# The low halves of one weight split of each gate and up pair, subtracted on GpSimd and not on VectorE

## The chip, the cores and the metric

The kernel runs on one core of one Trainium2 chip. The metric is device time in microseconds (us) of one execution; the time before is the median of three runs. Engine names are short: PE is TensorE (PEld its weight loads), DVE is VectorE, ACT is ScalarE, POOL is GpSimd, SP is SyncE, which issues most transfers.

## The reference

The network is a decoder trunk of two layers over 512 tokens of width 1024, in float32. Each layer has a mixer (a diagonal state space model, S5, beside chunked retention), a cross attention to a memory of 256 tokens, and a SwiGLU feed-forward part (FFN) of width 2816. The change concerns the last:

```python
D_MODEL, SEQ, DEPTH = 1024, 512, 2
D_FF = 2816

def rms_norm(x, g):
    y = x * lax.rsqrt(jnp.mean(x * x, axis=-1, keepdims=True) + EPS)
    return y * g

def swiglu(h, w_gate, w_up, w_down):
    return (jax.nn.silu(h @ w_gate) * (h @ w_up)) @ w_down

for l in range(DEPTH):
    ...                      # mixer, cross attention
    h = rms_norm(x, norm_ffn[l])
    x = x + swiglu(h, w_gate[l], w_up[l], w_down[l])
return rms_norm(x, norm_final)
```

## The kernel before

Activations lie transposed: 128 channels on the partitions, the 512 tokens along the free side. The matmuls run in a reduced form of float32 (fp32r), so every operand is split in two: a high part, which is the value copied to fp32r on ACT, and a low part, the value minus the high part, which DVE subtracts. A product takes three matmuls: high by high, high by low, low by high.

The FFN goes over its 2816 columns in four parts per layer (`FPARTS`: three of 6 blocks of 128 columns and one of 4). In a part the gate and up projections come first, then the down projection of the same columns. Gate and up use a Strassen-like scheme with seven products in place of eight: two neighbouring blocks of columns make a *pair* (one `gate` key and one `up` key for every two blocks, so 6 pairs in a part of 6 blocks, 4 in one of 4, 44 in the whole program). The sums of the weights that this scheme needs are formed on chip, in `prep_pair`, from two transfers `a` and `b` of 128 by 1024 each. Out of them come four *weight splits*, each a high and a low tile: `wa` (from `a`), `wb` (from `b`), `wc` (half as wide, from a sum) and `wd` (from another sum). For a pair DVE does four additions or subtractions of 128x512 on the raw tiles (shown as `raw<-raw` or `raw<-raw,raw`), three low parts of 128x1024 and one of 128x512 (`w<-raw,w`). ACT does the four high parts (`w<-raw`).

`pair_steps` then runs seven steps of 12 matmuls of 128x256, 84 for a pair (`ps<-u_nff,w`). Steps 0 and 1 read `wa`, 2 and 3 `wb`, 4 `wc`, 5 and 6 `wd`. `run_pairs` weaves the pairs into each other: the first three steps of the next pair stand between the last ones of this pair. After the steps, results are gathered from PSUM by ACT and DVE (`keep`: `u_gs<-ps,u_gs`, `u_us<-ps,u_us`), and the gating is done on DVE and ACT (`gated`, `merged`).

Buffers set what can run ahead: five tiles `raw` and eight tiles `w` of 128x1024. One pair takes all eight `w`, in a fixed turn, so a split of the next pair can be prepared only when PE has let go of the same split of this one.

The order of instructions on each engine isn't written by hand. The program records all operations, and a planner (`Program.schedule`) sorts them by due times, from a price for each operation (`price`: for a `tensor_tensor` on POOL 365 + 2.2 ns per element, on DVE 68 + 1.042 ns). Each engine then runs its list strictly in that order and waits on semaphores. Nothing in the prices ties one engine's duration to another's.

All instructions are issued at one helper (line 405 in the profile), so the rows tell operations apart by tile names. POOL has little to do: constants, S5 scalars at the start, S5 buffers and transfers in the mixers and in the FFN of the first layer, and four multiplications of the output (`u_fin`) at the end.

Of the kernel before, what the change touches and what calls it, by code (L numbers as in the profile page):

```python
# [10 lines left out]
F32 = mybir.dt.float32  # L11
# [406 lines left out]
def trunk(ctx, tc, io):  # L418
    nc = tc.nc
    mul, add, sub = ALU.mult, ALU.add, ALU.subtract  # L420
# [20 lines left out]
    V, S, G = Engine(prog, "DVE"), Engine(prog, "ACT"), Engine(prog, "POOL")  # L441
# [10 lines left out]
    def gen(s, dt=F32):  # L452
        return prog.buf("u", s, dt)
# [47 lines left out]
            finish()  # L501
        return ready.pop(i)

    def parts_of(x, s, n):
        hi, lo = prog.buf("w", s + "h"), prog.buf("w", s + "l")
        S.activation(out=hi[:, :n], in_=x, func=AF.Copy)
        V.tensor_tensor(out=lo[:, :n], in0=x, in1=hi.bitcast(F32)[:, :n], op=sub)
        return hi, lo

    def prep_pair(at):  # L510

        i = place[at]
        h = 512
        a, b = prog.buf("raw", "pa"), prog.buf("raw", "pb")
        Q.dma_start(out=a, in_=io["ws"][i, 0])
        Q.dma_start(out=b, in_=io["ws"][i, 1])
        V.tensor_tensor(out=b[:, :h], in0=b[:, :h], in1=b[:, h:], op=add)
        wa = parts_of(a, "wa", 2 * h)  # L520
        wb = parts_of(b, "wb", 2 * h)
        finish()
        V.tensor_tensor(out=b[:, :h], in0=b[:, :h], in1=a[:, :h], op=add)
        V.tensor_tensor(out=a[:, :h], in0=b[:, :h], in1=b[:, h:], op=sub)
        wc = parts_of(b[:, :h], "wc", h)

        def last():
            V.tensor_tensor(out=a[:, h:], in0=a[:, h:], in1=b[:, :h], op=add)
            ready[at] = (wa, wb, wc, parts_of(a, "wd", 2 * h))
        held.append(last)  # L530

    def finish():
        while held:
            held.pop()()
# [106 lines left out]
    for i in range(KT):  # L641
        Q.dma_start(out=xs[i], in_=io["xT"][:, i, :])
        raw, hi, lo = gen("w0")[:, :256], gen("w0h", F32R)[:, :256], gen("w0l", F32R)[:, :256]
# [1161 lines left out]
```

## Time and profile before

| quantity | before |
|---|---|
| median of 3 runs | 1473.82 us (1472.47 to 1475.63) |
| profiled execution, its own time | 1476.17 us |
| its span, first to last instruction | 1474.4 us |
| PE busy, of the span | 1453.7 us (99%) |
| DVE busy | 1192.1 us (81%) |
| ACT busy | 798.6 us (54%) |
| POOL busy | 97.9 us (7%) |
| TensorE clock granted, mean | 0.995 of full speed |

Busy shares are means over stages that differ. The table by windows cuts the span into stretches and gives the busy time and number of instructions of each engine in each; the table of groups gives the mean duration of one instruction of a kind. Consecutive instructions of DVE and of POOL overlap by some 0.05 to 0.1 us in the records, so what one instruction costs its engine is the distance from its start to the next start. Spans on POOL are called rough by the page, one more reason to go by the distances between starts. "ps" is a tile in PSUM, all other tiles lie in SBUF.

### The profile page before, as it was taken

The page shows a single profiled execution, that of the slowest core. Times are in us where ns is not written, and L with a number is a line of the kernel's source. Part 1 is how long each engine was busy: PE and PEld are TensorE (multiplying, and loading weights), DVE is VectorE, ACT ScalarE, POOL GpSimd, SP SyncE. Part 2 cuts the span into 40 slices and gives each one's busy share as a digit, 9 for nine tenths or more (in the row PEclk, how much of TensorE's full clock was granted, in tenths as well). Part 3 has the DMA queues.
Part 4 walks back from the last instruction along what each step waited for, and adds up shares of the span by engine and source line. Part 5 has one row for each costly group of instructions (what it writes and reads, how often), then busy time and mean ns, then how long its engine had stood idle before and what let it go on. Part 6 is the DMA issues. An engine that isn't in the chain of part 4 may idle for free.

```text
span 1474.4 us, 23052 instructions
## 1 busy us (share of the span) xinstructions
PE 1453.7 (99%) x8784; PEld 1279.2 (87%) x8784; DVE 1192.1 (81%) x2072; ACT 798.6 (54%) x1375; POOL 97.9 (7%) x201
## 2 busy tenths in 40 slices
PE   8999999999999999999999999999999999999997
PEld 6888788888898998998988888888889989999897
DVE  8799996576899797997963989756679969869596
ACT  5887665444665463564645436544455626436264
POOL 5721000000001001011000000000000000000001
PEclk8999999999999999999999999999999999999999
DMA  7534534221134334244345453332121322413321
GB/s 256 155 89 106 178 131 151 100 72 58 44 118 150 106 124 139 87 153 151 132 148 172 145 164 124 134 129 86 58 72 60 117 96 87 151 55 125 100 87 58
DMA packets 67023, 171.95 MB, mean 117 GB/s; under 512 B 11232, under 2 KB 22880, under 8 KB 66912
## 3 DMA queue, kind: packets, MB, share of 16 engines
q1 hardware_dynamic: 63808, 159.98, 32.4%
q0 software_dynamic: 3104, 10.49, 2.6%
q8 instruction: 69, 1.13, 0.3%
q14 instruction: 42, 0.34, 0.1%
HBM read 156.02 MB, written 13.63 MB: 115 GB/s over the span
## 4 chain that ended last, share of the span: by engine, by line
PE 82%; DVE 12%; ACT 3%; issue 1%; DMA 0%; SPq 0%; DVEq 0%; ACTq 0%
PE ps L405 82%; DVE w L405 3%; DVE u_gs L405 1%; DVE raw L405 1%; ACT w L405 1%; DVE u_us L405 1%; DVE s L405 1%; DVE u_gw L405 1%; DMA x<-in_xT_dram 0%; DVE u_mt L405 0%; ACT u_vc L405 0%; DVE u_rr L405 0%; ACT u_v L405 0%; SPq L405 0%; DVE u_ry L405 0%
## 5 line engine op out<-in xcount | busy, mean ns | idle before, releaser
L405 ACT ACTIVATE w<-raw 128x1024 fp32r<-128x1024 f32 (+1 forms) x348 | 347.8, 1003 | 414.9 <-PE ps L405 339.8
L405 PE MATMUL ps<-u_nff,w 128*128 128x256 f32 x3696 | 440.6, 280 | 0.7 <-DVE w L405 0.5
L405 PEld LDWEIGHTS ps<-u_nff,w 128*128 128x128 f32 x3696 | 436.9, 188 | 4.7 <-DVE w L405 1.9
L405 DVE TENSOR_TENSOR w<-raw,w 128x1024 fp32r<-128x1024 f32 (+1 forms) x336 | 383.7, 1148 | 55.7 <-ACT w L405 55.3
L405 PE MATMUL ps<-u_acth,w 128*128 128x512 f32 (+1 forms) x768 | 223.7, 375 | 0.0
L405 PEld LDWEIGHTS ps<-u_acth,w 128*128 128x128 f32 x768 | 139.9, 188 | 26.3
L405 PE MATMUL ps<-u_nmh,w 128*128 128x512 f32 x480 | 158.5, 402 | 0.0
L405 PE MATMUL ps<-u_actl,w 128*128 128x512 f32 (+1 forms) x384 | 143.0, 376 | 0.4 <-DVE u_actl L405 0.4
L405 DVE TENSOR_TENSOR x<-ps,x 128x512 f32<-128x512 f32 x88 | 60.5, 688 | 100.8 <-PE ps L405 100.5
L405 PEld LDWEIGHTS ps<-u_nmh,w 128*128 128x128 f32 x480 | 91.3, 191 | 18.7
L405 PE MATMUL ps<-u_nml,w 128*128 128x512 f32 x240 | 95.6, 398 | 0.0
L405 PEld LDWEIGHTS ps<-u_actl,w 128*128 128x128 f32 x384 | 72.2, 188 | 14.4 <-DVE u_actl L405 1.4
L405 PE MATMUL ps<-u_nch,w 128*128 128x512 f32 x256 | 81.7, 393 | 0.0
L405 PE MATMUL ps<-u_xoh,w 128*128 128x512 f32 x256 | 80.7, 392 | 0.0
L405 DVE TENSOR_TENSOR raw<-raw 128x512 f32<-128x512 f32 x88 | 60.4, 687 | 7.5 <-DMA raw<-in_ws_dram 7.0
L405 DVE TENSOR_TENSOR raw<-raw,raw 128x512 f32<-128x512 f32 x88 | 60.1, 683 | 0.4
L405 DVE TENSOR_TENSOR u_gs<-u_gs,u_nfry 128x512 f32<-128x512 f32 x88 | 59.0, 681 | 0.3
L405 PEld LDWEIGHTS ps<-u_nch,w 128*128 128x128 f32 x256 | 48.1, 188 | 10.4
L405 POOL TENSOR_TENSOR u_fin<-u_lp,u_lbc 128x512 f32<-128x512 f32 x4 | 5.4, 1392 | 775.3 <-ACT u_lbc L405 775.3
L405 PEld LDWEIGHTS ps<-u_xoh,w 128*128 128x128 f32 x256 | 48.0, 188 | 9.9
L405 PEld LDWEIGHTS ps<-u_nml,w 128*128 128x128 f32 x240 | 45.8, 191 | 9.4
L405 PE MATMUL ps<-u_xol,w 128*128 128x512 f32 x128 | 50.4, 393 | 0.0
(368 smaller groups left out, 2466.0 us busy)
## 6 DMA issues: line engine op xcount, KB each, us to landing
raw<-in_w_dram SPq DMA_DIRECT2D x166, 512.0 KB, 3.4
raw<-in_ws_dram SPq DMA_DIRECT2D x88, 512.0 KB, 3.5
u_s5x<-sp SPq DMA_DIRECT2D x28, 256.0 KB, 4.1
w<-in_w_dram POOLq DMA_DIRECT2D x6, 512.0 KB, 6.9
u_mr<-in_memT_dram SPq DMA_DIRECT2D x12, 256.0 KB, 4.7
x<-in_xT_dram SPq DMA_DIRECT2D x8, 256.0 KB, 4.7
tu<-u_u SPq DMA_DIRECT2D x8, 256.0 KB, 3.8
u_ub<-tu SPq DMA_DIRECT2D x32, 64.0 KB, 3.5
```

The source lines that it names most:

```text
L405: getattr(engines[o.eng], o.fn)(**k)
```

## The change

`parts_of` gets an optional engine for the subtraction that makes the low part, and `prep_pair` passes POOL for the first split of each pair, `wa`. The high parts stay on ACT, the other three low parts on DVE.

```diff
-    def parts_of(x, s, n):
+    def parts_of(x, s, n, eng=None):
         hi, lo = prog.buf("w", s + "h"), prog.buf("w", s + "l")
         S.activation(out=hi[:, :n], in_=x, func=AF.Copy)
-        V.tensor_tensor(out=lo[:, :n], in0=x, in1=hi.bitcast(F32)[:, :n], op=sub)
+        (eng or V).tensor_tensor(out=lo[:, :n], in0=x, in1=hi.bitcast(F32)[:, :n], op=sub)
         return hi, lo
...
-        wa = parts_of(a, "wa", 2 * h)
+        wa = parts_of(a, "wa", 2 * h, G)
         wb = parts_of(b, "wb", 2 * h)
```

Since the planner prices the two engines differently, the order on all engines shifts in the FFN. In the rows below a tile's name carries its buffer's number, as in `w_113` or `raw_105`. On DVE, in the third part of the second layer's FFN (some 1318 to 1327 us in the trace), the second pair to be prepared has `raw_105` as its `a` and `raw_106` as its `b`. Before:

```order
L405 TENSOR_TENSOR u_us<-ps_116,u_us 128x256 [waits PE_49,Activation_49]
L405 TENSOR_TENSOR u_gs<-u_gs,u_nfry 128x512 [waits Activation_49]
L405 TENSOR_TENSOR w_113<-raw_105,w_112 128x1024 [waits DMAHW4_49,Activation_49]
L405 TENSOR_TENSOR w_109<-raw_106,w_108 128x1024 [waits PE_49,Activation_49]
L405 TENSOR_TENSOR raw_107<-raw_107 128x512 [waits DMAHW7_49]
L405 TENSOR_TENSOR raw_106<-raw_106,raw_105 128x512 [waits DVE_49]
L405 SCALAR_TENSOR_TENSOR u_gs<-ps_122,u_gs 128x512
L405 TENSOR_TENSOR w_111<-raw_103,w_110 128x1024 [waits PE_49,Activation_49]
L405 TENSOR_TENSOR raw_105<-raw_106 128x512 [waits DVE_49]
L405 TENSOR_TENSOR w_115<-raw_106,w_114 128x512 [waits PE_49,Activation_49]
```

And with the change, DVE at the same place:

```order
L405 TENSOR_TENSOR u_us<-ps_121,u_us 128x256 [waits PE_49,Activation_49]
L405 TENSOR_TENSOR u_gs<-u_gs,u_nfry 128x512 [waits Activation_49]
L405 SCALAR_TENSOR_TENSOR u_gs<-ps_122,u_gs 128x512 [waits PE_49]
L405 TENSOR_TENSOR u_gs<-u_gs,u_nfry 128x512 [waits DVE_49]
L405 TENSOR_TENSOR w_109<-raw_106,w_108 128x1024 [waits Activation_49]
L405 TENSOR_TENSOR raw_107<-raw_107 128x512 [waits DMAHW7_49]
L405 TENSOR_TENSOR raw_106<-raw_106,raw_105 128x512 [waits DMAHW4_49,DVE_49]
L405 TENSOR_TENSOR u_gs<-u_gs,u_nfry 128x512 [waits Activation_49]
L405 TENSOR_TENSOR w_111<-raw_103,w_110 128x1024 [waits PE_49,Activation_49]
L405 TENSOR_TENSOR raw_105<-raw_106 128x512 [waits DVE_49,Pool_49]
L405 TENSOR_TENSOR w_115<-raw_106,w_114 128x512 [waits PE_49,Activation_49]
```

The low part `w_113<-raw_105,w_112` has left DVE, two gating operations on `u_gs` have moved up into its place, and the write into `raw_105`, which POOL now reads, waits for POOL as well.

On POOL, at the border between the FFN of the first layer (after its last S5 transfer) and that of the second, the difference reads as follows (+ is new; before, nothing stood there up to the `u_fin` of the end):

```order
 L405 DMA sp_207<-u_dt 128x512
+L405 TENSOR_TENSOR w_110<-raw_103,w_111 128x1024
+L405 TENSOR_TENSOR w_110<-raw_105,w_111 128x1024
+L405 TENSOR_TENSOR w_110<-raw_106,w_111 128x1024
+L405 TENSOR_TENSOR w_109<-raw_107,w_108 128x1024
+L405 TENSOR_TENSOR w_115<-raw_104,w_114 128x1024
```

Each is the low part of one pair's `wa`; there are 44 of them in all.

## Rows read from the trace of the kernel before

**Rows 1.** The page's first part: busy time by engine.
```profile
PE 1453.7 (99%) x8784; PEld 1279.2 (87%) x8784; DVE 1192.1 (81%) x2072; ACT 798.6 (54%) x1375; POOL 97.9 (7%) x201
```

**Rows 2.** Windows inside the eight gate and up stages: length, engines' busy us.
```profile
405.00:455.00 50.00, 49.79 (x416) 49.01 (x415) 49.20 (x74) 32.84 (x56) 1.68 (x4) 1.00 0.37 123
...
692.00:725.00 33.00, 33.00 (x285) 33.00 (x284) 30.95 (x44) 19.89 (x34) 0.00 (x0) 1.00 0.33 115
...
1223.00:1273.00 50.00, 50.00 (x423) 49.73 (x422) 48.20 (x71) 30.30 (x49) 0.00 (x0) 1.00 0.38 128
...
1410.00:1440.00 30.00, 30.00 (x256) 30.00 (x255) 28.87 (x41) 18.30 (x29) 0.00 (x0) 1.00 0.30 104
sum 368.00, PE 367.32 PEld 364.03 DVE 358.48 ACT 230.53 POOL 3.66; mean PE 45.91 PEld 45.50 DVE 44.81 ACT 28.82 POOL 0.46
```

**Rows 3.** Head of the chain of waits over 1307 to 1367 us.
```profile
by line: PE ps L405 40.3%; DVE w L405 22.8%; DVE raw L405 11.2%; issue 9.6%; DVE u_gs L405 7.8%; DVE u_us L405 6.5%; DVE u_actl L405 1.6%; ACT w L405 0.1%; DVEq L405 0.1%; ACTq L405 0.0%
```

**Rows 4.** DVE in order of time from 1324 us: start, duration.
```profile
1324.02 1.21 DVE L405 TENSOR_TENSOR w<-raw,w 128x1024 fp32r<-128x1024 f32 x1
1325.15 0.68 DVE L405 TENSOR_TENSOR raw<-raw 128x512 f32<-128x512 f32 x1
```

**Rows 5.** POOL's own two-input operations, in order of time: start, duration.
```profile
62.17 0.62 POOL L405 TENSOR_TENSOR u_s5bb<-u_s5b,fr 128x256 f32<-128x256 f32 x1
62.75 0.62 POOL L405 TENSOR_TENSOR u_s5bt<-u_s5b,fi 128x256 f32<-128x256 f32 x1
...
1456.91 1.30 POOL L405 TENSOR_TENSOR u_fin<-u_lp,u_lbc 128x512 f32<-128x512 f32 x1 [775.34 <-ACT u_lbc L405]
1458.16 1.30 POOL L405 TENSOR_TENSOR u_fin<-u_lp,u_lbc 128x512 f32<-128x512 f32 x1
1459.41 1.49 POOL L405 TENSOR_TENSOR u_fin<-u_lp,u_lbc 128x512 f32<-128x512 f32 x1
1460.87 1.48 POOL L405 TENSOR_TENSOR u_fin<-u_lp,u_lbc 128x512 f32<-128x512 f32 x1
```

**Rows 6.** DVE beside those four `u_fin`, in order of time.
```profile
1458.44 1.30 DVE L405 TENSOR_TENSOR u_la<-u_la,u_lq 128x256 f32<-128x256 f32 x1 [0.48 <-ACT u_lq L405]
1459.67 0.41 DVE L405 TENSOR_TENSOR u_ly<-ps,x 128x256 f32<-128x256 f32 x1
1460.56 0.63 DVE L405 TENSOR_TENSOR u_la<-u_la,u_lq 128x256 f32<-128x256 f32 x1 [0.48 <-ACT u_lq L405]
...
1463.50 0.42 DVE L405 TENSOR_TENSOR u_la<-u_la,u_lq 128x256 f32<-128x256 f32 x1 [0.55 <-ACT u_lq L405]
```

**Rows 7.** A POOL operation inside a gate and up stage, and DVE beside it.
```profile
413.73 0.61 POOL L405 TENSOR_TENSOR u_diag<-s5d,eye 32x256 f32<-32x256 f32 x1
413.84 1.06 DVE L405 TENSOR_TENSOR raw<-raw 128x512 f32<-128x512 f32 x1
```

**Rows 8.** POOL and DVE waiting for each other in the first mixer.
```profile
63.59 2.58 DVE L405 SCALAR_TENSOR_TENSOR s<-s,gam 128x4 f32<-128x4 f32 x1 [0.78 <-ACT u_v L405]
65.28 0.87 POOL L405 TENSOR_TENSOR u_s5bt<-u_s5b,fi 128x256 f32<-128x256 f32 x1
66.22 1.83 POOL L405 TENSOR_TENSOR u_s5bb<-u_s5bb,u_s5bt 128x256 f32<-128x256 f32 x1
66.25 1.21 DVE L405 TENSOR_TENSOR w<-raw,w 128x1024 fp32r<-128x1024 f32 x1
```

**Rows 9.** DVE's groups that read PSUM, 1223 to 1273 us: count, busy, mean ns.
```profile
L405 DVE TENSOR_TENSOR u_us<-ps,u_us 128x256 f32<-128x256 f32 x6 | 2.5, 417 | 0.4 <-PE ps L405 0.3
L405 DVE TENSOR_TENSOR u_gs<-ps,u_gs 128x256 f32<-128x256 f32 x5 | 2.1, 415 | 1.0 <-PE ps L405 1.0
L405 DVE SCALAR_TENSOR_TENSOR u_gs<-ps,u_gs 128x512 f32<-128x512 f32 x3 | 2.0, 680 | 0.0
L405 DVE SCALAR_TENSOR_TENSOR u_us<-ps,u_us 128x512 f32<-128x512 f32 x2 | 1.4, 679 | 0.0
```

**Rows 10.** The pairs' matmuls over the whole span.
```profile
L405 PE MATMUL ps<-u_nff,w 128*128 128x256 f32 x3696 | 440.6, 280 | 0.7 <-DVE w L405 0.5
```

## The prediction

> **What bounds the kernel now.** I read the page's busy times first. PE is busy for 99% of the span, DVE for 81% [rows 1]. Taken alone, this says that PE sets the time and DVE has a fifth to spare, so that relief for DVE is worth little and a burden on it costs little. But both are means over unlike stages, and the change works only in the gate and up stages of the FFN. So I laid a window inside each of the eight. Together the windows are 368.00 us long; in them DVE is busy for 358.48 us, 97%, and idle for 9.52 us, while POOL works for 3.66 us [rows 2]. ACT, with 230.53 us, is no bound. The reader is to see that the fifth of DVE's time that is free lies elsewhere, in the down projections and the attention.
>
> Then I asked which wait ends last there. In the third part of the second layer the chain runs 40.3% through PE, but 22.8% through DVE's low parts (`w`), 11.2% through its weight sums (`raw`), and 15.9% through gating (`u_gs`, `u_us`, `u_actl`) [rows 3]. DVE carries half of the path while PE is hardly idle: the two are level. One pair costs PE 84 matmuls, at the best pace of the windows (285 in 33.00 us, 0.1158 us each [rows 2]) 9.73 us, and DVE has about 9.5 us of work in the same time (48.20 us in a window of 423 matmuls, five pairs). What DVE gains or loses per pair therefore counts in very different ways. A gain meets PE at once: all 3696 matmuls of the pairs take 440.6 us [rows 10] and at the best pace would take 428.0, so no relief here is worth more than 12.6 us. A loss counts nearly in full.
>
> **What leaves DVE.** One low part of 128x1024 per pair, 44 in all. From its start to the next start is 1.13 us [rows 4], so DVE sheds 1.13 us per pair.
>
> **What POOL takes on.** The same subtraction, 44 times. Before, POOL has no operation of 128x1024. Uncontended it has two of 128x512 at 1.25 us from start to start and one of 128x256 at 0.58 us [rows 5]. Four times the small one is 2.32 us, twice the large one 2.50, and the line through both ends at 2.59. The third `u_fin`, which shared its time with DVE, took 1.46 from start to start, doubled 2.92: the upper end. I take 2.55, between the two readings that start at the nearest size. For POOL's own load this is nothing (2.55 in 9.73 us), and its queue is nearly empty there; in the first layer S5 buffers and transfers stand between the new operations, but they fall into the down stages.
>
> The Trainium skill has another price for this step. Its page "GPSIMD Engine Reference" (3.1, Elementwise) gives 4497 ns for an fp32 `tensor_tensor` of 2048 elements per partition; half of it, an estimate, is 2.25 us. By it the sum below would be 37 x (2.25 - 0.10 - 1.13) - 9.5 = 28 us; the trace's distances of 1.25 us for 512 elements speak for the dearer one.
>
> **What it does to DVE.** This decides. While POOL works through its four `u_fin`, DVE's `u_la`, which has two inputs in SBUF, takes 1.30 us in place of 0.42. It starts at 1458.44 and ends at 1459.74, 0.28 us after the second `u_fin` has ended at 1459.46. The next one takes 0.63 and again ends 0.29 us after a `u_fin` (1460.90). Between them `u_ly`, with one input in PSUM, takes its usual 0.41 in the midst of a `u_fin` [rows 5, 6]. It is no matter of that stage: at 413.84 us, inside a gate and up stage, a `raw<-raw` takes 1.06 us in place of 0.68 beside POOL's `u_diag` [rows 4, 7]. And it works both ways: POOL's `u_s5bb` of 128x256, started just before a low part on DVE, takes 1.83 us and ends 0.59 us after it [rows 8]. So a DVE operation with two SBUF inputs and a POOL operation that reads SBUF exclude each other, each for its whole length, and DVE, being in order, stands still behind its own head.
>
> The Trainium skill's page "SBUF — State Buffer" (Who interferes with whom) calls the port pair of the two an exclusive lock, held for the whole instruction, for exactly this combination. If the port were shared instead, each would slow in proportion, which is the first rival; the two `u_la` that end 0.28 us behind a `u_fin` fit the lock.
>
> In the gate and up stages nearly all of DVE's work is of the kind that is held: 16 of the 71 instructions of one window read PSUM, of 0.42 to 0.68 us [rows 2, 9]. When POOL gets its turn at the end of a DVE operation, the next one can run beside it with a chance of 16 in 71, for about 0.45 us, so 0.10 us per POOL operation is hidden. The rest of 2.55, 2.45 us, is lost to DVE. Per pair: 2.55 - 0.10 - 1.13 = 1.32 us more.
>
> **The sum.** The eight windows hold 3117 matmuls, 37 pairs. The other seven of the 44 are prepared in the stretch before a stage, where DVE has time. 37 x 1.32 = 48.8 us; the 9.5 us that DVE idles in the windows are taken to be used up first, which leaves 39.3. The lag can't be passed on to the down stage: the last pair's `u_actl` is an input of the first down products. The profiled execution took 1476.17 us (a span of 1474.4 and 1.8 around it); with 39 it is 1515. It lies 2.35 above the median of the runs, so I predict 1513 us, 2.7% more. With 2.32 and 2.92 for POOL the sum is 31 and 53 us, and with none of the idle time won back 49: 1505 to 1527.
>
> **The moved steps.** DMAs, SP's queue and ACT's high parts stay as many. DVE's write into `a` now waits for POOL. Behind that write stand `wc`'s low part and the sum for `wd`, and PE waits for these. I cost it at nothing, since three to five DVE operations stand between the two and DVE is held while POOL works anyway. If that cover is gone it is the third rival. The low part of `wa` itself comes 1.4 us later. PE needs it four steps of 12 matmuls after it has freed the buffer, 5.6 us; ACT's copy (1.06), a turn's wait and 2.55 fit into that.
>
> **The rivals.** First, no effect: POOL and DVE share and only part of the 2.55 us is lost. With half of it, 37 x (1.27 - 0.10 - 1.13) is 1.5 us, less than DVE's idle time, and the kernel stays at 1474. For it: only a few pairs of operations in the trace show the exclusion, on small tiles. Against it: none shows the contrary.
>
> Second, on the other side, faster: POOL reads only between DVE's operations without holding them, so that DVE loses 1.13 us of its 9.5 per pair and PE is the only bound. It pays from the point at which a POOL operation holds DVE for less than 1.13 us; the price is at most the 12.6 us of PE's lost pace, of which I would give it 8, 1466. For it: POOL has time, and the chain does lie on DVE's `w`. Against it: rows 6 and 7.
>
> Third, much slower: besides being held, DVE stands at the write into `a` because POOL had to wait for its own turn first. The `u_s5bb` waited 1.21 us for one DVE operation (1.83 - 0.62) [rows 5, 8]. If DVE loses such a turn once per pair, 37 x 1.13 = 42 us come on top: 1555. For it: the planner's prices know of no exclusion, so its order is too tight; and a DVE operation of 4 columns once took 2.58 us, until the third POOL operation behind which it stood was done [rows 8]. Against it: POOL has one operation per pair here, none back to back.
>
> **How the numbers follow.** The exclusion with DVE as the bound: 0.66. No effect: 0.09. Faster: 0.06. Much slower: 0.19. A measurement of this kernel can tell about 0.2%, 3 us. Slower by more takes the first, the last and a little of the second case, 0.87; within 0.2% 0.07; faster 0.06. The range goes from 1482, between no effect and the low end of the sum, to 1550, most of the way to the third rival: left out are the first two rivals and a part of the third, 0.2.
>
> **What would show it.** In the changed profile, DVE should lie at 97 to 100% of the gate and up stages with an unchanged amount of useful work: two-input operations on DVE, mostly of 0.68 and 1.22 us, should have members of 2 to 4 us, one per pair, each ending just after a POOL `w<-raw,w`, and those that read PSUM should not. POOL's new group should have 44 members of 2.6 us or, with its turn, up to 3.8, some 2.6 to 3.5 in the mean. PE should wait for `w` on DVE or POOL, with 84 matmuls taking some 10.9 us in place of 9.8, and the gate and up stages longer by 4 to 6 us each (those of 4 blocks by half of it). The down stages and everything outside the FFN should be as long as before. The prediction is wrong if DVE's two-input durations stay as they are, if its idle time there grows (then the wait for POOL is the cause and the third rival is the case), or if the loss sits in the down stages.

## The result, and the profile after

The changed kernel takes 1517.28 us (median of 4 runs, 1514.66 to 1519.31) against 1474.72 for the kernel before beside it (1472.47 to 1475.87): a ratio of 1.0289, interval 1.0277 to 1.0301, or 43 us slower. The forecast was 1513. The size is right and the exclusion of DVE and POOL is real, but the way from the one to the other is not the one forecast: DVE did not become the bound. Two terms were wrong in opposite directions, and most of the loss hangs on something for which the prediction's sum has no term: where DVE's stands fall in its list, and how little PE can run ahead of them. That 1513 came so near is in good part luck.

The profiled execution took 1517.59 us with a span of 1515.7. Its busy times (before: [rows 1]):

```profile
PE 1458.9 (96%) x8784; PEld 1281.9 (85%) x8784; DVE 1205.7 (80%) x2028; ACT 796.7 (53%) x1375; POOL 212.7 (14%) x245
```

DVE has 44 instructions fewer and is busy for 13.6 us more. That is the whole of DVE's added time, over the program; the span is 41.3 longer. Next, windows inside the gate and up stages, as in [rows 2] but where these stages lie now (length, busy us of PE, PEld, DVE, ACT, POOL, granted clock, DMA share, GB/s):

```profile
405.00:455.00 50.00, 44.88 (x373) 43.83 (x373) 47.35 (x68) 29.86 (x52) 13.85 (x10) 1.00 0.31 106
...
1347.00:1397.00 50.00, 44.88 (x364) 44.07 (x364) 44.71 (x60) 24.91 (x42) 9.65 (x4) 0.97 0.30 98
...
sum 363.00, PE 325.21 PEld 318.85 DVE 335.95 ACT 196.26 POOL 81.34; mean PE 40.65 PEld 39.86 DVE 41.99 ACT 24.53 POOL 10.17
```

PE, which was hardly ever idle here (0.68 of 368 us), now lacks 37.8 of 363 us. DVE, which should have filled up, has become less busy: it idles 27.1 of 363 us, where it idled 9.5 of 368. Both engines wait, by turns. The chain of the third part of the second layer, now 1338 to 1405 us, says the same (before: [rows 3]): PE's share rises from 40.3 to 51.9%, DVE's falls.

```profile
by line: PE ps L405 51.9%; DVE w L405 14.8%; issue 11.3%; DVE u_us L405 9.4%; DVE raw L405 5.6%; DVE u_gs L405 3.3%; DVE u_actl L405 2.1%; ACT u_acth L405 1.0%; ACT w L405 1.0%; DVEq L405 0.1%; ACTq L405 0.0%
```

The groups of the whole span (count, then busy us, mean ns of one, idle us before them and what ended it). On DVE, the operations of two SBUF inputs that meet POOL, and those that read PSUM (before: [rows 9]); then POOL's new group, and the pairs' matmuls (before: [rows 10]):

```profile
L405 DVE TENSOR_TENSOR u_gs<-u_gs,u_nfry 128x512 f32<-128x512 f32 x88 | 74.0, 849 | 1.3 <-ACT u_gs L405 0.2
L405 DVE TENSOR_TENSOR u_us<-u_us,u_gs 128x512 f32<-128x512 f32 x44 | 43.6, 1007 | 0.5
L405 DVE TENSOR_TENSOR u_gs<-ps,u_gs 128x256 f32<-128x256 f32 x44 | 18.5, 419 | 18.1 <-PE ps L405 18.0
L405 DVE TENSOR_TENSOR u_us<-ps,u_us 128x256 f32<-128x256 f32 x44 | 18.4, 418 | 6.6 <-PE ps L405 6.1
...
L405 POOL TENSOR_TENSOR w<-raw,w 128x1024 fp32r<-128x1024 f32 x44 | 110.9, 2521 | 1096.1 <-ACT w L405 1087.5 <-DVE u_gs L405 8.6
...
L405 PE MATMUL ps<-u_nff,w 128*128 128x256 f32 x3696 | 447.5, 281 | 40.8 <-DVE w L405 37.8 <-DVE u_nff L405 3.0
```

The first two groups took 0.68 us each before, as the profile before has it for the first of them:

```profile
L405 DVE TENSOR_TENSOR u_gs<-u_gs,u_nfry 128x512 f32<-128x512 f32 x88 | 59.0, 681 | 0.3
```

Their means have risen by the members that POOL holds. The PSUM readers keep their 0.42. PE stood 0.7 us before the pairs' matmuls; now it stands 40.8, of which 37.8 for `w` on DVE. The list of PE's waits (us, times, longest) shows how that is made up:

```profile
PE ps L405 <- DVE w L405: 38.5, 29, 2.3
```

29 waits of 1.3 us in the mean. The two engines in order of time show one of them (start, duration; in brackets the idle time before it and what ended it):

```profile
1362.30 0.69 DVE L405 SCALAR_TENSOR_TENSOR u_us<-ps,u_us 128x512 f32<-128x512 f32 x1
1362.65 2.41 POOL L405 TENSOR_TENSOR w<-raw,w 128x1024 fp32r<-128x1024 f32 x1 [9.19 <-ACT w L405]
1363.03 2.58 DVE L405 TENSOR_TENSOR u_us<-u_us,u_gs 128x512 f32<-128x512 f32 x1
...
1365.53 1.21 DVE L405 TENSOR_TENSOR w<-raw,w 128x1024 fp32r<-128x1024 f32 x1
...
1368.48 1.21 DVE L405 TENSOR_TENSOR w<-raw,w 128x1024 fp32r<-128x1024 f32 x1
...
1369.74 6.51 PE L405 MATMUL ps<-u_nff,w 128*128 128x256 f32 x40 [1.81 <-DVE w L405]
...
1373.86 0.43 DVE L405 TENSOR_TENSOR u_us<-ps,u_us 128x256 f32<-128x256 f32 x1 [1.30 <-PE ps L405]
```

POOL starts beside an operation that reads PSUM, which is not held. The next one, the gating `u_us<-u_us,u_gs`, stands until POOL's end at 1365.06 and is done 0.55 us after it: 1.90 us longer than usual. Behind it stand two low parts that PE needs; PE waits 1.81 us for the second. And because PE is late, DVE waits 1.30 us, six operations on, for a result in PSUM that isn't there yet. So this stand is paid twice: by PE, and by DVE's in-order list, which waits for PE.

### The profile page after: what moved, and what is told of

The parts are those of the page before. It is cut to its first block, busy times and chain, and to the rows that moved or that the text cites. A ratio compares the mean times of both kernels' runs of the same rounds, so it can differ in the third digit from the quotient of the medians.

```text
span 1515.7 us, 23157 instructions
## 1 busy us (share of the span) xinstructions
PE 1458.9 (96%) x8784; PEld 1281.9 (85%) x8784; DVE 1205.7 (80%) x2028; ACT 796.7 (53%) x1375; POOL 212.7 (14%) x245
## 3 DMA queue, kind: packets, MB, share of 16 engines
q8 instruction: 69, 1.13, 0.3%
## 4 chain that ended last, share of the span: by engine, by line
PE 75%; DVE 17%; issue 4%; ACT 3%; DMA 1%; SPq 0%; DVEq 0%; ACTq 0%
PE ps L405 75%; DVE w L405 5%; DVE raw L405 2%; DVE u_gs L405 2%; DVE u_us L405 2%; ACT w L405 1%; DVE s L405 1%; DVE u_gw L405 0%; DVE u_actl L405 0%; DMA raw<-in_w_dram 0%; ACT u_vc L405 0%; DVE u_mt L405 0%; DVE u_nfrt L405 0%; DVE u_mb L405 0%; DVE u_nfta L405 0%
## 5 line engine op out<-in xcount | busy, mean ns | idle before, releaser
L405 PE MATMUL ps<-u_nff,w 128*128 128x256 f32 x3696 | 447.5, 281 | 40.8 <-DVE w L405 37.8
L405 DVE TENSOR_TENSOR w<-raw,w 128x1024 fp32r<-128x1024 f32 (+1 forms) x292 | 332.8, 1146 | 57.4 <-ACT w L405 57.0
L405 POOL TENSOR_TENSOR w<-raw,w 128x1024 fp32r<-128x1024 f32 x44 | 110.9, 2521 | 1096.1 <-ACT w L405 1087.5
L405 DVE TENSOR_TENSOR u_gs<-u_gs,u_nfry 128x512 f32<-128x512 f32 x88 | 74.0, 849 | 1.3 <-ACT u_gs L405 0.2
L405 ACT ACTIVATE u_acth<-u_us 128x512 fp32r<-128x512 f32 x44 | 27.6, 629 | 51.4 <-DVE u_us L405 51.3
L405 ACT ACTIVATE u_gs<-u_gs 128x512 f32<-128x512 f32 x44 | 27.6, 628 | 51.0 <-DVE u_gs L405 50.9
```

What stands on the lines that cost most here:

```text
L405: getattr(engines[o.eng], o.fn)(**k)
```

## Experiments

Three questions were open: is it POOL's reading, or only that its result comes late? Is the cost DVE's time, or the order? And what was the relief worth?

**Only the order, and only the engine.** The first kernel has every instruction where the changed one has it, but issues the subtraction on DVE; the second has the order of before and issues it on POOL.

```diff
-                getattr(engines[o.eng], o.fn)(**k)
+                getattr(engines[o.on or o.eng], o.fn)(**k)
...
         wa = parts_of(a, "wa", 2 * h, G)    # second kernel: without G
+        prog.ops[-1].on = "DVE"             # second kernel: "POOL"
```

> The planner still believes that the low part of wa is on POOL, so the order of every engine is that of the changed kernel, but the subtraction is issued on DVE at its place in that order. Theory A (exclusion: a POOL operation that reads SBUF holds DVE) expects the loss to be gone: 1470 to 1478 us. Theory B (the new order, with gating ahead of the low parts, is what costs) expects most of the loss to stay: 1500 to 1517 us. Theory C (the low part of wa comes too late because POOL is slow, exclusion or not) expects 1470 to 1480 us.

> The reverse: the planner believes that the low part is on DVE, so the order is that of the kernel before, but the subtraction is issued on POOL. Theory A expects the loss to stay, 1505 to 1525 us, with DVE operations of 2 to 3 us beside POOL. Theory B expects it to be gone, 1470 to 1480 us. Theory C expects it to stay, 1500 to 1525 us.

Measured: 1500.93 us (1.0175, 1.016 to 1.019) for the order alone, 1496.72 (1.0147, 1.013 to 1.0164) for the engine alone. PE's waits for DVE's `w`, of the first and of the second kernel:

```profile
PE ps L405 <- DVE w L405: 28.1, 27, 1.5
```

```profile
PE ps L405 <- DVE w L405: 17.7, 29, 1.0
```

The first lies where theory B had it, the second meets no theory. Each half of the change costs over 20 us by itself, and the two together would be more than the whole (26 and 22 of 43). But the 26 are no price of the order alone: the order of after is made for a DVE that is rid of the subtraction and leaves no room for 1.13 us more per pair; with the subtraction off DVE, the same order costs nothing (the fills below). In the order of before the standing falls mostly on low parts (these DVE operations took 1.22 us before):

```profile
L405 DVE TENSOR_TENSOR w<-raw,w 128x1024 fp32r<-128x1024 f32 x248 | 326.6, 1320 | 67.5 <-ACT w L405 66.9
```

**POOL without its read.** In the order of after POOL subtracts one column and fills the rest of the low tile with zeros, in three fills (some 1.15 us) or in seven (2.3 us).

```diff
+            if getattr(o, "on", None):
+                e, n = engines["POOL"], 342
+                e.tensor_tensor(out=k["out"][:, :1], in0=k["in0"][:, :1], in1=k["in1"][:, :1], op=k["op"])
+                for c in range(3):          # second kernel: (0, 1, 2, 0, 1, 2, 0)
+                    e.memset(k["out"].bitcast(F32)[:, 1 + c * 341:342 + c * 341], 0.0)
...
```

> The changed kernel, its order kept, but POOL reads only one column of a and of the high part and then fills the low part of wa with zeros by three memsets (the subtraction is left out), about as long as the subtraction. PE still waits for POOL, but POOL hardly reads SBUF. Theory A expects DVE's durations to be back at 0.68 and 1.22 us, and the time to be that of before or a little less: 1463 to 1476 us. Theory B expects the loss to stay: 1505 to 1517 us. Theory C expects it to stay: 1500 to 1517 us.

> In e3 POOL's substitute took only some 1.15 us a pair (0.12 and three fills of 0.3), half of the subtraction's 2.41, so e3 could not rule out that the low part is simply late. Here seven fills make it some 2.3 us long, again with one column read and the subtraction left out. Theory A (exclusion) expects e3's time again, 1467 to 1473 us. Theory C (POOL's low part comes too late for PE) expects 1490 to 1517 us and PE waiting for POOL's w.

Measured: 1470.17 us (0.9969, 0.9957 to 0.9981) and 1470.80 (0.9969, 0.9959 to 0.998), both as theory A had it. The second one in order of time:

```profile
1344.88 0.69 DVE L410 SCALAR_TENSOR_TENSOR u_us<-ps,u_us 128x512 f32<-128x512 f32 x1
1345.04 0.19 POOL L404 TENSOR_TENSOR w<-raw,w 128x1 fp32r<-128x1 f32 x1 [7.41 <-ACT w L410]
1345.17 2.34 POOL L406 MEMSET w<- 128x341 f32 x7
1345.61 0.69 DVE L410 TENSOR_TENSOR u_us<-u_us,u_gs 128x512 f32<-128x512 f32 x1
1346.22 1.22 DVE L410 TENSOR_TENSOR w<-raw,w 128x1024 fp32r<-128x1024 f32 x1
1347.36 0.68 DVE L410 TENSOR_TENSOR u_actl<-u_us,u_acth 128x512 fp32r<-128x512 f32 x1
```

The list of DVE is the changed kernel's, instruction by instruction; this is the place two pairs on from the one shown above, and there the changed kernel's `u_us<-u_us,u_gs` took 2.43 us (at 1386.90). POOL works as long as there. But three operations of DVE run beside the fills at their usual 0.69 and 1.22 us, and PE doesn't wait. So a low part that is late by this much is no cause; the read is. The write into `a` is not tested by it, since it waits only for the one column that is read; but in the changed kernel's own list of waits no operation of DVE waits for POOL's `w`. The two also give the worth of the relief alone: 0.3%, 4.6 and 4.1 us. And they give the standing by itself: the changed kernel, with the same DVE instructions in the same order, has DVE busy for 1205.7 us, this one for 1151.5. The 54 us between them are 1.23 us per pair.

DVE's waits for PSUM are in the list itself, stands or no stands. Before the gathers they are nearly as long here as in the changed kernel (17.7 against 18.0 us; 7.9 in the kernel before), so that over the program the second payment of a stand is small:

```profile
L410 DVE TENSOR_TENSOR u_gs<-ps,u_gs 128x256 f32<-128x256 f32 x44 | 18.5, 420 | 17.7 <-PE ps L410 17.7
```

**The read alone.** The kernel before, and beside each low part of `wa`, which stays on DVE, POOL reads 128x768 for an output that nobody waits for.

```diff
+            if o.on:
+                out, one = self.idle
+                engines["POOL"].tensor_tensor(
+                    out=out, in0=one.unsqueeze(1).to_broadcast([P, 6, P]), op=ALU.add,
+                    in1=k["in1"][:, :6 * P].rearrange("p (a t) -> p a t", a=6))
...
```

> The kernel before in its own order with the subtraction on DVE, and beside each low part of wa one POOL operation of 128x768 with two inputs in SBUF whose result (into a bf16 tile of its own) nobody waits for. Theory A as it was predicted (DVE loses the whole length of the POOL operation, 0.75 x 2.45 = 1.84 us a pair, and is relieved of nothing) expects 37 x 1.84 - 9.5 = 58 us more, 1533 us. Theory A with the shorter hold that the changed kernel shows (its two-input operations grew by 37 us in all, 0.84 us a pair) expects 20 to 35 us more, 1495 to 1510 us. Theories B and C expect no change: 1470 to 1480 us.

Measured: 1518.96 us (1.0295, 1.028 to 1.0311). DVE's low parts, POOL's reads, the pairs' matmuls:

```profile
L410 DVE TENSOR_TENSOR w<-raw,w 128x1024 fp32r<-128x1024 f32 x292 | 397.9, 1367 | 52.2 <-ACT w L410 51.9
...
L404 POOL TENSOR_TENSOR idle<-ident,w 128x768 bf16<-128x768 f32 x44 | 121.8, 2769 | 1079.0 <-ACT w L410 684.1 <-DVE u_nff L410 394.9
...
L410 PE MATMUL ps<-u_nff,w 128*128 128x256 f32 x3696 | 447.2, 281 | 39.3 <-DVE w L410 36.2 <-DVE u_nff L410 2.7
```

A read that has no consumer makes PE wait 39.3 us, nearly as much as the change (40.8). DVE is busy for 56.8 us more (1248.9 against 1192.1), 1.29 per pair. The time lies between the two forecasts of theory A: for 768 columns POOL's operation took 2.77 us in the mean, more than the 2.52 of the subtraction and not three quarters of it, and nothing was taken off DVE.

**The read in two pieces.** Is it the sum of DVE's standing that costs, or that a single stand is long? Halves make the single one shorter.

```diff
+        for c in range(0, n, n // 2 if eng else n):
+            d = c + (n // 2 if eng else n)
+            (eng or V).tensor_tensor(out=lo[:, c:d], in0=x[:, c:d], in1=hi.bitcast(F32)[:, c:d], op=sub)
```

> The changed kernel with POOL's subtraction cut into two of 512 columns, so that DVE can get a turn between them and no single stand of DVE is longer than 1.3 us. Theory A1 (what costs is the sum of DVE's standing, a rate) expects about the same sum and time, 1510 to 1522 us. Theory A2 (what costs is that one long stand delays the next low parts on DVE's list by more than the buffers give) expects a clear part of the loss back: 1490 to 1505 us.

Measured: 1516.79 us (1.0283, 1.0259 to 1.0307), no better. In order of time:

```profile
1363.51 3.02 POOL L405 TENSOR_TENSOR w<-raw,w 128x512 fp32r<-128x512 f32 x2 [8.59 <-ACT w L405]
1364.04 1.33 DVE L405 TENSOR_TENSOR u_us<-u_us,u_gs 128x512 f32<-128x512 f32 x1
1365.29 2.33 DVE L405 TENSOR_TENSOR w<-raw,w 128x1024 fp32r<-128x1024 f32 x1
```

DVE gets its turn between the halves and stands twice, 0.65 and 1.1 us. Over the program the sum is the same: DVE is busy for 1204.1 us, in the changed kernel for 1205.7.

**The planner knows of the standing.** The planner counts DVE as occupied for 1.7 us from when it places POOL's subtraction.

```diff
+                if e == "POOL" and o.fn == "tensor_tensor" and o.dur > 2000:
+                    clock["DVE"] = max(clock["DVE"], t) + HELD    # HELD = 1700
```

> The changed kernel, but the planner is told: when it places a low part on POOL it counts DVE as occupied for 1.7 us from then on. Theory A1 (DVE's sum) expects little, 1510 to 1517 us, since the work and the standing stay. Theory A2 together with the order (DVE's relief was planned away to gating ahead of the low parts, so a stand meets a list without slack) expects about half of the loss back, as in e2 with the order of before: 1485 to 1500 us.

Measured: 1493.10 us (1.0119, 1.0101 to 1.0137). In order of time:

```profile
1345.03 2.42 POOL L408 TENSOR_TENSOR w<-raw,w 128x1024 fp32r<-128x1024 f32 x1 [8.45 <-ACT w L408]
1346.46 2.07 DVE L408 TENSOR_TENSOR w<-raw,w 128x1024 fp32r<-128x1024 f32 x1 [0.99 <-ACT w L408]
```

POOL now starts where DVE waits for ACT for 0.99 us anyway, and the stand is 0.86 us. Of the 43 us, 24 are gone with the same work on every engine, as the theory that put the cost down to the order expected.

**More slack.** Ten tiles `w` in place of eight, for four tiles `u`, in the changed kernel and in that of before.

```diff
-"u": 58, "s": 40, "raw": 5, "w": 8
+"u": 54, "s": 40, "raw": 5, "w": 10
```

> The changed kernel with ten weight tiles w in place of eight (paid for with four tiles u), so that splits of the next pair can be prepared earlier. Theory L (DVE's list, standing and all, still fits into a pair's time on PE; what costs is that each standing comes just before a split that PE needs, because the eight tiles leave no slack): most of the loss goes, 1478 to 1492 us, PE's wait for w on DVE falls below 15 us. Theory T (DVE's throughput is the bound, as the prediction had it: work plus standing is more than PE's time for a pair): no amount of slack helps, 1510 to 1518 us, and DVE is busy for the whole of the gate and up stages.

> The kernel before with ten tiles w in place of eight, the same four tiles u given up: what the extra slack is worth without the standing. Both theories: 1466 to 1477 us. By theory L the gain is small, since PE hardly waits for w before (0.7 us); if it is as large as that of the run on the changed kernel, the slack has nothing to do with the standing.

Measured: 1502.58 us (1.0194, 1.018 to 1.0207) and 1469.55 (0.9965, 0.9952 to 0.9979). The changed kernel's pair matmuls:

```profile
L405 PE MATMUL ps<-u_nff,w 128*128 128x256 f32 x3696 | 441.3, 280 | 20.3 <-DVE w L405 11.4 <-ACT u_us L405 7.4 <-ACT u_gs L405 1.2
```

Neither theory was met: the slack brings 14.7 us back, 10 more than it brings the kernel before, but not most of the loss. PE's wait for `w` falls from 37.8 to 11.4 us, and a wait for ACT's results appears in part of its place.

**Both remedies.**

> The changed kernel with both remedies: the planner counts DVE as occupied for 1.7 us when it places GpSimd's subtraction (alone 1493.1 us), and ten tiles w in place of eight (alone 1502.6 us, against 1469.6 for the kernel before with ten). GpSimd's work and its reads are the same 44 of 128x1024. If the standing costs only through what it makes late (order and buffers without slack), the two add up: 1474 to 1484 us, the loss almost gone, though DVE still stands. If DVE's throughput sets a floor (its own work plus 1.2 to 1.7 us of standing is more than PE's 9.8 us a pair), the second remedy brings little: 1488 us or more, DVE at 97 to 100% of the gate and up stages.

Measured: 1477.16 us (1.0015, 1.0005 to 1.0024). The windows, laid into its stages, their sum; the head of the chain of the third part of the second layer, 1308 to 1368 us; the pairs' matmuls; and one of POOL's subtractions with DVE beside it:

```profile
sum 363.00, PE 359.55 PEld 357.97 DVE 330.98 ACT 215.47 POOL 88.49; mean PE 44.94 PEld 44.75 DVE 41.37 ACT 26.93 POOL 11.06
```

```profile
by line: PE ps L408 75.8%; DVE w L408 8.9%; DVE u_gs L408 6.7%; issue 4.5%; DVE u_us L408 3.4%; DVE raw L408 1.2%; DVE u_actl L408 1.1%; DVEq L408 0.1%
```

```profile
L408 PE MATMUL ps<-u_nff,w 128*128 128x256 f32 x3696 | 437.0, 279 | 1.7 <-ACT w L408 1.3 <-ACT u_us L408 0.2
```

```profile
1346.12 2.41 POOL L408 TENSOR_TENSOR w<-raw,w 128x1024 fp32r<-128x1024 f32 x1 [6.65 <-ACT w L408]
1346.16 0.68 DVE L408 SCALAR_TENSOR_TENSOR u_gs<-ps,u_gs 128x512 f32<-128x512 f32 x1
1346.76 2.32 DVE L408 TENSOR_TENSOR raw<-raw,raw 128x512 f32<-128x512 f32 x1
```

This is what the first of the two forecasts had, and it decides the second question. POOL does the same 44 subtractions, DVE still stands (here 1.64 us longer than usual), and DVE is as busy in the windows as in the changed kernel (91% and 93%). But PE waits 1.7 us in place of 40.8, and the loss is 2.6 us. What the standing still costs is seen against the kernel before with the same ten tiles: 7.6 us, between two separate runs. So some 35 of the 43 us hang on where the stand falls and on the want of slack. The stand itself is shorter here too, though not by as much: DVE is busy for 1180.4 us, and in that other kernel for 1187.1, of which 49.7 (44 times 1.13) would be shed; the 43 us between are 0.98 per pair, against 1.23. So shorter stands and better places come together here, and what each is worth isn't shown apart.

**The relief without a read.** Two kernels take DVE's work off in another way, with a transfer issued by POOL that adds to its target. In the first ACT writes minus the high part of `wa`, and the transfer adds the weights; in the second, the first of the weight sums of `b` is formed so, and all low parts stay on DVE.

```diff
-        wa = parts_of(a, "wa", 2 * h)
+        wa = prog.buf("w", "wah"), prog.buf("w", "wal")
+        S.activation(out=wa[0], in_=a, func=AF.Copy)
+        S.activation(out=wa[1], in_=a, func=AF.Copy, scale=-1.0)
+        G.dma_start(out=wa[1], in_=io["ws"][i, 0].bitcast(F32R), accum_op=add)
```

```diff
-        V.tensor_tensor(out=b[:, :h], in0=b[:, :h], in1=b[:, h:], op=add)
+        G.dma_start(out=b[:, :h], in_=io["ws"][i, 1][:, h:], accum_op=add)
```

> The kernel before, with the low part of the first split of a pair formed without DVE and without a POOL operation that reads SBUF: ACT writes minus the high part into the low tile, and a transfer issued by POOL adds the weights to it from memory. DVE sheds the same 1.13 us per pair as in the change. Theory of the exclusion (POOL's read is what costs, the relief alone is worth 4 to 5 us): 1468 to 1473 us, DVE's two-input operations at their usual 0.68 and 1.22 us, PE's wait for w below 2 us. Rival (any later arrival of this low part costs, or the writes of the transfer into SBUF hold DVE too): 1480 us or more.

> The kernel before, with the first of a pair's weight sums (b, 128x512) formed by a transfer issued by POOL that adds the second half to the first from memory, not by DVE. DVE sheds some 0.6 us per pair, 26 us in all. Theory that DVE's relief is worth little, since PE is at its pace: 1470 to 1474 us. Rival (the added transfer comes too late for the high part of the second split, on which three steps wait): 1478 us or more, with PE waiting for w on ACT or DVE.

Measured: 1482.90 us (1.0061, 1.0047 to 1.0074) and 1470.19 (0.9977, 0.9969 to 0.9986). The pairs' matmuls of the first:

```profile
L405 PE MATMUL ps<-u_nff,w 128*128 128x256 f32 x3696 | 448.1, 281 | 4.3 <-DVE w L405 2.6 <-DMA w<-in_ws_dram 0.9 <-ACT w L405 0.4
```

The first expectation failed. DVE's two-input operations there take their usual time (0.68 and 1.22 us), so nothing holds DVE, but the pairs' matmuls take 7.5 us more in all, with little idle time shown between them. A matmul lasts 0.28 us in the records and the next starts after 0.12, so that short waits don't show as idle. The weight loads, which run ahead of the matmuls, do show them; first this kernel, then the kernel before:

```profile
L405 PEld LDWEIGHTS ps<-u_nff,w 128*128 128x128 f32 x3696 | 440.6, 188 | 12.3 <-DMA w<-in_ws_dram 5.0 <-DVE w L405 3.4 <-ACT w L405 0.8
...
L405 PEld LDWEIGHTS ps<-u_nff,w 128*128 128x128 f32 x3696 | 436.9, 188 | 4.7 <-DVE w L405 1.9
```

The largest part is the wait for the landing of the transfer, which comes 5.4 us after its issue (median). The distances from one matmul's start to the next agree: their median is 0.118 us in both kernels, so PE's own pace is the same, but 133 of them are over 0.13 us where 47 were, 16.3 us beyond the usual in place of 5.4. So a low part that comes later than that of the fills does cost, in short waits, as the first half of the rival had it.

The second kernel came out as forecast, and is faster than the kernel before by 3.6 us, 0.2%, near the bound of what can be told. Ten tiles `w` gave as much, and the two weren't run together.

## Why the prediction was right, and where it was wrong

**The exclusion: right.** Held operations of 2 to 4 us that end just after POOL's `w<-raw,w`, PSUM readers untouched, were forecast and are there (31 of 2.0 to 2.9 us, where 44 were forecast, one per pair); without the read they vanish, and with the read alone they come. The Trainium skill's page "SBUF — State Buffer" (SBUF: two separate sides) calls it an exclusive lock for the whole instruction: the `u_us` that is done 0.55 us behind POOL's end fits it, as do the two stands beside the two halves.

**POOL's duration: right within 0.15 us.** 2.55 was taken from the trace's small sizes; the median of the 44 is 2.416, so it was 0.13 too high. The 2.25, an estimate from the "GPSIMD Engine Reference" (3.1, Elementwise) of the Trainium skill, is 0.17 too low.

**The hold, 2.45 us per pair: twice too large.** It is 1.23 (the change against the kernel of the seven fills) to 1.29 (the read alone). The step that failed is "with a chance of 16 in 71, for about 0.45 us": POOL gets its turn at the end of an operation, and that is often where DVE idles, or starts one that reads PSUM of 0.69 us. Such cover was costed at 0.10 and is over a microsecond. Read one by one in the trace, 34 of POOL's 44 operations hold one of DVE, by 1.62 us in the mean; the other ten, all just before a stage or at its head, find DVE idle for most of their time. Of POOL's 110.9 us in all, 25.5 lie where DVE idles and 20.7 beside its PSUM readers.

**DVE as the bound: wrong.** The prediction had "the two are level", so that a loss on DVE "counts nearly in full", and summed 1.32 us of DVE time per pair to 48.8 us. Measured, it is otherwise. Shed 1.13 and held 1.23, DVE gains next to nothing per pair, some 5 us in all; its busy time rises by 13.6 us in the program, since the order of after alone, with the subtraction on DVE, already brings 8.6 (1200.7 us). No sum of DVE's time reaches 43. The signature of 97 to 100% failed (92.5%), and the prediction's own sign of error, DVE's idle time growing, came true. It had put that to the third rival, the wait at the write into `a`. That isn't it: DVE's list of waits names no `w` of POOL, and what ended its idle time in these stages is mostly PE (18.0 us before `u_gs<-ps,u_gs` alone). Where nothing is taken off DVE, the working holds better: the read alone brought DVE 57 us, and with the 9.5 of idle time taken off that is 47, against 44 measured.

**The moved steps: the largest term, and it was missing.** The prediction weighed only the new wait at the write into `a`, which is nothing, as costed; not that the planner puts gating in front of the low parts because it thinks DVE free. In the order of after, the stand falls just ahead of low parts that PE needs within a few steps, and eight tiles `w` let nothing run ahead. Telling the planner gives back 24 us, and two more tiles 16 on top (the kernel before gains 4 from them too).

**The relief: "no relief here is worth more than 12.6 us" holds.** It is worth 4 to 5. But the sum then netted it at its full 1.13 us per pair, 42 us. With the measured 1.23 in place of 2.45 the same sum gives 37 x 0.10 = 4 us, less than DVE's idle time, and so no loss at all. The hold at twice its size took the place of the missing term, and that the two are nearly equal is luck.

**The stages: nearly.** The part shown takes 67 us (1338 to 1405) in place of 60, 11.1 us per pair where 10.9 were forecast. From first to last pair matmul the eight stages together are 45 us longer (495.8 against 450.7), those of six pairs by 5 to 8 where 4 to 6 were forecast, and the rest of the program is 4 us shorter.

## What to carry to other kernels

Before moving a two-input operation from VectorE to GpSimd, ask not what VectorE sheds but which of its operations will stand behind GpSimd's read, and who waits for that one: here a hold of about the length of the work shed cost 43 us or 3 (8 against the kernel before with the same buffers), by where it fell and what could run ahead. If a planner sets the order, give it the hold as a price and give the consumer buffers to run ahead, before judging the move. And an engine that is busy 97% of a stage need not be its bound: test it by taking work off it alone (here 0.3%) before summing its time into a forecast. Adding time to it is another test with another answer (here 57 us on it cost 44).

## What the runs showed of the hardware

Fills on GpSimd don't hold VectorE: 2.34 us of them ran beside three operations at their usual durations, where a two-input operation of 2.41 us in the changed kernel held one for 1.90.

Two GpSimd operations in a row didn't shut VectorE out for their whole length: it had its turn between the halves (1.33 us, then 2.33), so cutting the read into pieces neither helped nor hurt.

A wait of PE of 1.81 us (it ended at 1369.74) was followed by a stretch at the lower of TensorE's two clock levels, 1.2 GHz and not 2.4, within the stage (the granted clock stands last but two in each row; it was 1.00 in the rest of 1338 to 1396 but for these four us; the last row is the next microsecond):

```profile
1371.00:1372.00 1.00, 1.00 (x7) 1.00 (x6) 0.96 (x3) 0.00 (x0) 0.00 (x0) 0.53 0.91 336
...
1374.00:1375.00 1.00, 1.00 (x8) 1.00 (x8) 0.88 (x2) 0.69 (x1) 0.24 (x1) 0.76 0.36 139
1375.00:1376.00 1.00, 1.00 (x11) 1.00 (x10) 0.42 (x1) 0.48 (x1) 1.00 (x1) 1.00 0.02 8
```

Seven matmuls fall into a microsecond there, eleven into one at the higher level. It happened in two of the eight stages, the other time right behind a wait of 2.00 us that ended at 1292.54. Not every such wait was followed by it: one of 2.32 us that ended at 440.56 was not. A mean of 0.97 over 50 us is 1.5 us of PE's time each, an estimate, 3 of the 43.
